# Key stage of an RWKV-7 / GLA trunk: matrix order fixed by hand, head sums on quarters of the array, low-rank results kept on chip

## The chip, the cores and the metric

The kernel runs on one core of a Trainium2 chip. A core has a matrix engine (PE, with its weight loads listed apart as PEld), three elementwise engines (DVE for tensor arithmetic, ACT for activations and copies, POOL), and a queue (SP) from which this kernel issues its DMA transfers. The metric is the device time of one execution in microseconds. Three runs of the kernel before gave 2408.81 to 2409.78 us, median 2409.51 us.

## The reference

Two layers over 272 tokens (16 learned ones and 256 given) of width 2048: RWKV-7 time mixing, then gated linear attention, each followed by a squared-ReLU MLP. The change lies in the first layer, where each of 32 heads has 64 channels:

```python
r = xr @ w_rkv[0]
k = xk @ w_rkv[1]
w_log = -softplus(-(w0 + tanh(xw @ w1) @ w2)) - 0.5
a = sigmoid(a0 + (xa @ a1) @ a2)
kk = hs(k * k_k)                                    # hs: split into heads of 64
kk = kk / maximum(sqrt(sum(kk * kk, axis=-1)), 1e-12)
k = k * (1.0 + (a - 1.0) * k_a)
decay = exp(-exp(hs(w_log)))
y = rwkv7_scan(rh, decay, kh, vh, -kk, kk * ah)
bonus = (sum(rh * kh * r_k, axis=-1, keepdims=True) * vh)
```

Two sums over the 64 channels of a head are needed per token: that of `kk * kk`, which normalizes the key, and that of `rh * kh * r_k`, the bonus.

## The kernel before, in words

Activations are held transposed: 128 channels (two heads) on the partitions, 272 tokens along the row, 16 such tiles. A weight block of 128x1024 float32 is fetched as `raw` (L131, three buffers), split by ACT into a high part `hi` (L137) and by DVE into the rest `lo` (L138), two buffers of each, and used in eight steps of three matmuls (L160 to L162: hi times high part, hi times rest, lo times high part). A projection tile is two blocks, so 48 matmuls into one bank of the accumulator, called `pj` or, for every third tile of keys, `pry`.

Stages of the first layer: receptance (`r`) projections; between them, for each tile, the low-rank results (function `lora`: two small matmuls, L468 and L469, two sigmoids, a scan), which are written to a DRAM tensor `cad` and read back in the key stage (`ca`, L565); then the key stage, the loop over 16 tiles; then the value projections with the chunked recurrence interleaved.

In the key stage a tile f does this. PE makes the 48 matmuls. ACT makes `kk` (key times k_k, L569), its square `sq` (L570), two exponentials `W` and `iW` of the scanned decay (L567, L568), and `kn` (L571). PE sums `sq` over the heads with a 128x128 block matrix of ones, `bones` (L573, into `pm`); ACT takes logarithm and exponential of that (L574, L575); DVE normalizes (L577) and fills, by `put`, the two slots of the tiles `bk` and `ar` (two buffers each): slot 0 of `ar` from `kk`, slot 1 from `r` times `W`, slot 0 of `bk` from `kn`, slot 1 from `kk`. These go to DRAM (`bkd`, L583; `ard`, L586). DVE makes r times k times r_k (L584), PE sums it (L588, into `pu`), ACT copies the sum over `r` (L589). After tile 7 the first 256 columns of tiles 0 to 7 come back as `BK0` and `AR0` (`fetch`, L504), from tile 10 on `scores` multiplies them (L518), with masks on DVE, and after tile 13 `invert`, some 60 dependent DVE operations (`upd`, `sysA`), solves the triangular systems.

The order: outside the blocks marked `manual_schedule` a scheduler lays out every engine's instructions ahead of time, by priority (weight loads first, then program order) and its own estimates of readiness; each engine then runs its list strictly in that order, and waits where an operand is late. In the key stage before, all engines are laid out so, PE too. In the value stage PE's order is written by hand.

Of the kernel before, what the change touches and what calls it, by code (L numbers as in the profile page):

```python
# [11 lines left out]
F32R = mybir.dt.float32r  # L12
# [42 lines left out]
class Kern:  # L55
# [235 lines left out]
    def rwkv(self, done):  # L291
# [193 lines left out]
        tc.keep_in_program_order(nc.scalar.preload_act_table_set("natural_log_exp_and_others"))  # L485
# [4 lines left out]
        nc.gpsimd.memset(Wf[:, 0:1], 1.0)  # L490
        W = Wf[:, 1:]
# [68 lines left out]
        for f in range(KT):  # L560
            r = rr[f]
# [4 lines left out]
            iW, kk, sq, kn = (self.t(ep, [P, T], n, 2) for n in ("iW", "kk", "sq", "kn"))  # L566
            nc.scalar.activation(W, ca[:, 0], AF.Exp, scale=-DECAY)  # L567
            nc.scalar.activation(iW, ca[:, 0], AF.Exp, scale=DECAY)  # L568
            nc.scalar.mul(self.two(kk), ps, self.vec("k_k", f))  # L569
            nc.scalar.activation(sq, kk, AF.Square)  # L570
            nc.scalar.activation(kn, ca[:, 1], AF.Identity, scale=self.vec("k_a", f), bias=self.omka[:, f : f + 1])  # L571
            ss = self.pm()[:, :T]
            nc.tensor.matmul(ss, self.bones, sq, start=True, stop=True)  # L573
            nc.scalar.activation(sq, ss, AF.Ln, bias=self.tiny)  # L574
            nc.scalar.activation(sq, sq, AF.Exp, scale=-0.5)  # L575
            tt(self.two(kn), ps, self.two(kn))
            nc.vector.scalar_tensor_tensor(out=kk, in0=sq, scalar=1e12, in1=kk, op0=ALU.min, op1=ALU.mult)  # L577
            put(ar, 0, kk, Wf[:, :T], 1)
            nc.vector.tensor_copy(ar[:, 0:513:128], kk[:, ::C])
            tt(kk, kk, ca[:, 1])  # L580
            put(bk, 1, kk, iW)
            put(bk, 0, kn, iW)
            nc.sync.dma_start(bkd[f], bk)  # L583
            nc.vector.scalar_tensor_tensor(out=kn, in0=r, scalar=self.vec("r_k", f), in1=kn, op0=ALU.mult, op1=ALU.mult)  # L584
            put(ar, 1, r, W)
            nc.sync.dma_start(ard[f], ar)  # L586
            rk = self.pu()[:, :T]
            nc.tensor.matmul(rk, self.bones, kn, start=True, stop=True)  # L588
            nc.scalar.copy(r, rk)  # L589
            nc.vector.tensor_copy(WC[:, f], W[:, C - 1 : 4 * C : C])  # L590
            if f == 0:
                xv = mix(3, self.xp)
                early2.close()
                wl = ExitStack()
                lp = wl.enter_context(tc.tile_pool(name="wl", bufs=1, reuse_waits="tile"))
                BKs, ARs = ([self.t(lp, [P, 8, 256], n)] for n in ("BK0", "AR0"))
                AMs, AMrs = [self.t(lp, [P, 2, 16, 128], "AM0")], []
                sysA = self.t(lp, [P, 32, 32], "sysA")
                t11 = sysA.rearrange("p a b -> p (a b)")[64:96].rearrange("p (c h s) -> p c h s", c=2, h=16)
                nc.gpsimd.memset(sysA, 0.0)  # L600
            if f == 7:
                fetch(0, BKs, bkd)
                fetch(0, ARs, ard)
            if 9 < f < 14:
                scores(0, (f - 10) // 2, f % 2)
            if f == 13:
                inv = invert(0)
            if f > 13:
                for _ in range(6):
                    next(inv, None)  # L610
# [4 lines left out]
        BKs.append(self.t(kp, [P, 8, 320], "BK1"))  # L615
# [269 lines left out]
        units1 = ((2, 0), (2, 1), (3, 0), (3, 1), (4, 0))  # L885
        self.split_parts = 2
        for i in ((0, 128), (128, 320)):
            fetch(1, BKs, bkd, i)
# [417 lines left out]
```

## Time and profile before

| | us |
|---|---|
| median of three runs | 2409.51 |
| profiled execution, its own time | 2414.07 |
| span of its profile | 2412.3 |
| PE busy in the span | 2364.2 |
| DVE busy | 1636.8 |
| ACT busy | 1239.3 |
| PE busy from 157 to 291 us (the key stage) | 123.87 of 134.00 |
| DVE busy there | 110.91 |
| ACT busy there | 89.79 |

A page of the profile lists each engine's busy time, the chain of work that ended last, the costliest groups of instructions, and the DMA issues. Timeline rows give the start, the length and the engine of single instructions, and in brackets the engine's idle time before one and what ended it. Since matmuls overlap in the pipeline, their cost on PE is read from start to start, not from their lengths. A float32 matmul appears as two records.

### The profile page before, as it was taken

What the parts mean: (1) busy time and instruction counts of PE and PEld (TensorE: products, weight loads), DVE (VectorE), ACT (ScalarE), POOL (GpSimd) and SP (SyncE); (2) the same over time, 40 slices, a digit from 0 to 9 for tenths busy, and PEclk for the clock granted to TensorE, in tenths of its full rate; (3) what the DMA queues carried; (4) which work ended last, traced back from release to release, by engine and by line L of the source; (5) the groups of instructions that cost most, each with busy time, mean ns of one, the idle gap of its engine ahead of it and who ended that gap; (6) DMA issues with size and microseconds to landing.
All of it is one profiled execution on the core that took longest, in us unless ns stands there. A gap on an engine that the chain in (4) does not pass through costs nothing.

```text
span 2412.3 us, 47144 instructions
## 1 busy us (share of the span) xinstructions
PE 2364.2 (98%) x19257; PEld 2233.8 (93%) x19257; DVE 1636.8 (68%) x2742; ACT 1239.3 (51%) x1951; POOL 6.6 (0%) x20
## 2 busy tenths in 40 slices
PE   9999999899999999999999999999999999999998
PEld 8888888789999999999999989998999999999997
DVE  8777886858655555555556788778766666666666
ACT  6366544456555445445445565545555545445444
POOL 0000000000000000000000000000000000000000
PEclk9999999999999999999999999999999999999999
DMA  6578765534555655555555554555666666666665
GB/s 211 170 233 284 240 191 147 148 88 155 183 192 188 190 191 189 188 191 192 187 190 192 182 172 161 166 166 180 197 201 201 201 202 201 202 201 201 201 201 172
DMA packets 160729, 455.29 MB, mean 189 GB/s; under 512 B 34112, under 2 KB 50624, under 8 KB 160512
## 3 DMA queue, kind: packets, MB, share of 16 engines
q1 hardware_dynamic: 160512, 452.27, 58.2%
q8 instruction: 151, 2.47, 0.4%
q14 instruction: 66, 0.54, 0.1%
HBM read 433.86 MB, written 18.35 MB: 187 GB/s over the span
## 4 chain that ended last, share of the span: by engine, by line
PE 70%; DVE 3%; ACT 1%; issue 0%; DVEq 0%; ACTq 0%
PE pj L189 23%; PE pj L160 12%; PE pj L162 12%; PE pj L161 12%; PE pj L190 11%; DVE lo L138 1%; PE pt L1091 0%; DVE sg L1150 0%; ACT hi L137 0%; PE pu L1103 0%; PE pt L1123 0%; DVE cum L1027 0%; DVE fin L1213 0%; PE pu L1104 0%; DVE cj L200 0%
## 5 line engine op out<-in xcount | busy, mean ns | idle before, releaser
L137 ACT CAST hi<-raw 128x1024 fp32r<-128x1024 f32 (+1 forms) x818 | 794.5, 979 | 951.4 <-PE pj L161 514.9
L138 DVE TENSOR_TENSOR lo<-raw,hi 128x1024 fp32r<-128x1024 f32 (+1 forms) x818 | 926.5, 1139 | 518.8 <-ACT hi L137 510.2
L160 PE MATMUL pj<-x,hi 128*128 128x272 f32 x2240 | 642.0, 287 | 5.7 <-DVE cj L200 4.0
L162 PE MATMUL pj<-x,lo 128*128 128x272 f32 x2240 | 629.1, 281 | 4.6 <-DVE lo L138 4.3
L161 PE MATMUL pj<-x,hi 128*128 128x272 f32 x2240 | 628.3, 280 | 0.2 <-DVE x L233 0.2
L189 PE MATMUL pj<-x,hi 128*128 128x512 f32 x1664 | 550.0, 384 | 2.3 <-DVE cj L200 1.3
L190 PE MATMUL pj<-x,lo 128*128 128x256 f32 x1664 | 455.8, 274 | 2.3 <-DVE lo L138 2.2
L160 PEld LDWEIGHTS pj<-x,hi 128*128 128x128 f32 x2240 | 424.2, 189 | 13.7 <-issue 3.7
L162 PEld LDWEIGHTS pj<-x,lo 128*128 128x128 f32 x2240 | 424.4, 189 | 8.0 <-DVE lo L138 7.3
L161 PEld LDWEIGHTS pj<-x,hi 128*128 128x128 f32 x2240 | 424.5, 190 | 3.6 <-issue 1.4
L189 PEld LDWEIGHTS pj<-x,hi 128*128 128x128 f32 x1664 | 315.4, 190 | 46.0 <-ACT hi L137 2.9
L189 PE MATMUL pj<-h,hi 128*128 128x512 f32 x1008 | 330.3, 382 | 0.0
L190 PEld LDWEIGHTS pj<-x,lo 128*128 128x128 f32 x1664 | 320.1, 192 | 6.8 <-DVE lo L138 6.3
L160 PE MATMUL pj<-h,hi 128*128 128x272 f32 (+1 forms) x1040 | 290.1, 279 | 0.0
L161 PE MATMUL pj<-h,hi 128*128 128x272 f32 (+1 forms) x1040 | 290.1, 279 | 0.0
L162 PE MATMUL pj<-h,lo 128*128 128x272 f32 (+1 forms) x1040 | 290.1, 279 | 0.0
L190 PE MATMUL pj<-h,lo 128*128 128x256 f32 x1008 | 274.8, 273 | 0.0
L189 PEld LDWEIGHTS pj<-h,hi 128*128 128x128 f32 x1008 | 190.5, 189 | 26.4
L160 PEld LDWEIGHTS pj<-h,hi 128*128 128x128 f32 x1040 | 196.6, 189 | 0.0
L161 PEld LDWEIGHTS pj<-h,hi 128*128 128x128 f32 x1040 | 196.6, 189 | 0.0
L162 PEld LDWEIGHTS pj<-h,lo 128*128 128x128 f32 x1040 | 196.6, 189 | 0.0
L190 PEld LDWEIGHTS pj<-h,lo 128*128 128x128 f32 x1008 | 193.5, 192 | 0.0
(268 smaller groups left out, 2110.5 us busy)
## 6 DMA issues: line engine op xcount, KB each, us to landing
raw<-mlp_w_d SPq DMA_DIRECT2D x512, 512.0 KB, 4.2
raw<-gla_in_d SPq DMA_DIRECT2D x98, 512.0 KB, 3.4
raw<-w_rkv_d SPq DMA_DIRECT2D x80, 512.0 KB, 4.1
raw<-gla_o_d SPq DMA_DIRECT2D x32, 512.0 KB, 4.2
raw<-w_r_d SPq DMA_DIRECT2D x16, 512.0 KB, 3.4
raw<-rw_oQ_d SPq DMA_DIRECT2D x16, 512.0 KB, 3.4
ard<-ar SPq DMA_DIRECT2D x16, 288.0 KB, 3.6
bkd<-bk SPq DMA_DIRECT2D x16, 288.0 KB, 4.3
```

The costliest lines, as they stand in the source:

```text
L137: nc.scalar.copy(hi[:, h], raw[:, h])
L138: nc.vector.tensor_tensor(out=lo[:, h], in0=raw[:, h], in1=hi[:, h].bitcast(F32), op=ALU.subtract)
L160: nc.tensor.matmul(out, hi[:, ws], xh, start=first, stop=False)
L161: nc.tensor.matmul(out, hi[:, ws], xl, start=False, stop=False)
L162: nc.tensor.matmul(out, lo[:, ws], xh, start=False, stop=last)
L189: nc.tensor.matmul(wide, hi[:, ws], xt, start=kt == 0, stop=False)
L190: nc.tensor.matmul(one, lo[:, ws], xt[:, 0], start=False, stop=kt == nk - 1)
```

## The change

1. In `lora` the results of tiles 0 to 7 are written straight into `hres`, an on-chip tensor that is free at that time; `cad` is written for tiles 8 to 15 alone, and each of these is read into `hres` by a transfer that tile f - 8 of the key stage issues.
2. The mixed input of the values is computed into `d` during the last receptance tiles, its split (`hl`) stays at key tile 1.
3. PE's order in the key stage is written by hand: first half of tile f's projection, the sums for tile f - 1 and f - 2, second half of tile f.
4. `sums` replaces the two 128x128 sums: for each of `sq` (of tile f - 1) and `kn` (of tile f - 2) two matmuls with 64x64 corners of `bones`. Those of `sq` lie on the array's two diagonal quarters, those of `kn` on the other two, so that the heads of `rk` come out swapped and two half copies put them back.
5. `W` gets two buffers; the copies into `ar` and `WC` move from DVE to ACT.
6. `store` writes the tiles 4 to 7 into `BK0`, `AR0` and `BK1` on chip; tiles 0 to 3 are fetched in three transfers after tiles 5, 6 and 7. `BK1` lies in a pool that is open by then, and its later fetch is gone. `scores` and `invert` start one tile earlier.

```diff
-            st = self.t(ep, [P, 2, T], "ca", 2)
+            st = hres[:, 2 * f : 2 * f + 2] if f < NR else self.t(ep, [P, 2, T], "ca", 2)
...
-            nc.sync.dma_start(cad[f], st.rearrange("p a t -> p (a t)"))
+            if f >= NR:
+                nc.sync.dma_start(cad[f], st.rearrange("p a t -> p (a t)"))
...
+            if f == KT - 2:
+                for kt in range(KT):
+                    mixed(d[:, kt], kt, 3)
...
-        Wf = self.t(ep, [P, T + 1], "W")
+        Wfs = [self.t(ep, [P, T + 1], "W", 2) for _ in range(2)]
...
+        def store(f, dst, x, i):
+            if 3 < f < 8:
+                nc.sync.dma_start((BKs, ARs)[i][0][:, f], x[:, :256])
+                nc.sync.dma_start(dst[f][:, 256:] if i else BKs[1][:, f], x[:, 256:])
+            else:
+                nc.sync.dma_start(dst[f], x)
...
+        def sums(sq):
+            ss, last = self.pm()[:, :T] if sq is not None else None, held.pop() if held else None
+            todo = [(sq, ss, 0)] if sq is not None else []
+            if last:
+                r, kn = last
+                rk = self.pu()[:, :T]
+                todo.append((kn, rk, 1))
+            for x, out, i in todo:
+                for q in range(2):
+                    nc.tensor.matmul(out[half(q ^ i)], self.bones[half(q), half(q)], x[half(q)], start=True, stop=True)
+            if last:
+                for q in range(2):
+                    nc.scalar.copy(r[half(q)], rk[half(1 - q)])
+            return ss
...
-            ps = self.proj(pair(wk, f), xk, T, bank=self.pry if f % 3 == 2 else None)
-            ca = self.t(ep, [P, 2, T], "ca", 2)
-            nc.sync.dma_start(ca.rearrange("p a t -> p (a t)"), cad[f])
...
+        def rest(f):
+            r, Wf = rr[f], Wfs[f % 2]
...
+            ca = hres[:, 2 * i : 2 * i + 2]
...
+            ss = sums(sq)
...
+            put(ar, 1, r, W)
...
+            held.append((r, kn))
...
-            nc.vector.tensor_copy(ar[:, 0:513:128], kk[:, ::C])
+            nc.scalar.copy(ar[:, 0:513:128], kk[:, ::C])
+            store(f, ard, ar, 1)
...
+            if f < NR:
+                nc.sync.dma_start(ca.rearrange("p a t -> p (a t)"), cad[f + NR])
+            store(f, bkd, bk, 0)
+            nc.scalar.copy(WC[:, f], W[:, C - 1 : 4 * C : C])
...
+        with tc.manual_schedule(engines={ENG.PE}):
+            for f in range(KT + 1):
+                if f < KT:
+                    ps = (self.pry if f % 3 == 2 else self.pj)()[:, :T]
+                    keyproj(f, ps, 0)
+                if f:
+                    rest(f - 1)
+                if f < KT:
+                    keyproj(f, ps, 1)
+                    front(f, ps)
...
+                if f in (5, 6, 7):
+                    dst, src, i, j = ((BKs[0], bkd, 0, 256), (ARs[0], ard, 0, 256), (BKs[1], bkd, 256, 576))[f - 5]
+                    nc.sync.dma_start(dst[:, :4], src[:4, :, i:j].rearrange("f p n -> p f n"))
+                if 8 < f < 13:
+                    scores(0, (f - 9) // 2, (f + 1) % 2)
+                if f == 12:
+                    inv = invert(0)
...
+            sums(None)
```

PE's list before, in the first half of key tile 5 (`pry`), with `sq` of tile 4:

```order
L160 MATMUL pry_2362<-x_1209,hi_2365 128x272
L161 MATMUL pry_2362<-x_1209,hi_2365 128x272
L162 MATMUL pry_2362<-x_1209,lo_2366 128x272
L573 MATMUL pm_2339<-sq_2332,cst_125 128x272
L160 MATMUL pry_2362<-x_1210,hi_2365 128x272
```

The sum stood after the fifth of the tile's sixteen groups of three; that over `kn` of the same tile stood inside the ninth. PE's list now, at the second half of key tile 5 (`pry`); the sums stand in the middle of the 48 matmuls, `pm` with `sq` of tile 4 and `pu` with `kn` of tile 3:

```order
L160 MATMUL pry_2308<-x_1212,hi_2311 128x272
L161 MATMUL pry_2308<-x_1212,hi_2311 128x272
L162 MATMUL pry_2308<-x_1212,lo_2312 128x272
L584 MATMUL pm_2343<-sq_2305,cst_125 64x272 x2
L584 MATMUL pu_2344<-kn_2243,cst_125 64x272 x2
L160 MATMUL pry_2308<-x_1213,hi_2375 128x272
L161 MATMUL pry_2308<-x_1213,hi_2375 128x272
L162 MATMUL pry_2308<-x_1213,lo_2376 128x272
```

Before, each tile had one instruction of each kind with 128 rows, at a place that the scheduler chose; now four of 64 rows stand together, at the same place in every tile.

DVE's list before, from the normalizing of key tile 4 (`kk_2331`) on; `ar_1791` is the buffer of tiles 3 and 5, `r_20` is the receptance of tile 5:

```order
L577 SCALAR_TENSOR_TENSOR kk_2331<-sq_2332,kk_2331 128x272
L293 TENSOR_TENSOR ar_1790<-kk_2331,W_1796 128x4x64
L293 TENSOR_TENSOR ar_1790<-kk_2331,W_1796 128x15
L579 COPY ar_1790<-kk_2331 128x5
L138 TENSOR_TENSOR lo_2461<-raw_2458,hi_2460 128x1024
L293 TENSOR_TENSOR kk_2331<-kk_2331,ca_2328 128x272
L293 TENSOR_TENSOR ar_1791<-r_20_94,W_1796 128x4x64
L293 TENSOR_TENSOR bk_1788<-kk_2331,iW_2330 128x4x64
L293 TENSOR_TENSOR bk_1788<-kk_2331,iW_2330 128x16
L293 TENSOR_TENSOR ar_1791<-r_20_94,W_1796 128x16
L590 COPY WC_105<-W_1796 128x4
L138 TENSOR_TENSOR lo_2491<-raw_2488,hi_2490 128x1024
```

The first write into the buffer of tile 3 for tile 5 (`ar_1791` from `r_20`) stood behind tile 4's normalizing, a whole tile's row of work after tile 3's.

DVE's list now, from the last products of tile 2 (`kk_2110`, which was stored from buffer `ar_1790`) to the normalizing of tile 3 (`kk_2207`); `r_19` is the receptance of tile 4, which uses `ar_1790` again:

```order
L293 TENSOR_TENSOR kk_2110<-kk_2110,hres_72 128x272
L293 TENSOR_TENSOR bk_1788<-kk_2110,iW_2145 128x4x64
L293 TENSOR_TENSOR bk_1788<-kk_2110,iW_2145 128x16
L138 TENSOR_TENSOR lo_2277<-raw_2274,hi_2276 128x1024
L293 TENSOR_TENSOR kn_2243<-pj_2114,kn_2243 128x272
L293 TENSOR_TENSOR ar_1790<-r_19_93,W_1796 128x4x64
L293 TENSOR_TENSOR bk_1789<-kn_2243,iW_2242 128x4x64
L293 TENSOR_TENSOR bk_1789<-kn_2243,iW_2242 128x16
L293 TENSOR_TENSOR ar_1790<-r_19_93,W_1796 128x16
L620 SCALAR_TENSOR_TENSOR kn_2243<-r_18_92,vecs_126,kn_2243 128x272
L138 TENSOR_TENSOR lo_2312<-raw_2309,hi_2311 128x1024
L622 SCALAR_TENSOR_TENSOR kk_2207<-sq_2208,kk_2207 128x272
```

The slot from `r` of tile 4 is now written ahead of tile 3's normalizing, into the buffer that tile 2 has just stored: between that store and this write stand three products, one weight split and one more product. The two small copies are gone from this list.

ACT's list now, in the low-rank stage, where `hres` takes the results of tiles 0 to 2 and `x` is the mixed input of the keys:

```order
L471 ACTIVATE iW_1301<-pm_1297,vecs_126 128x272
L329 CAST x_1220<-xm_1281 128x272
L472 ACTIVATE hres_72<-pry_1298,vecs_126 128x272
L614 ACT_TABLE_LOAD
L614 ACTIVATE W_1796<-hres_72 128x272
L471 ACT_TABLE_LOAD
L471 ACTIVATE iW_1311<-pm_1307,vecs_126 128x272
L137 CAST hi_1410<-raw_1408 128x1024
L472 ACTIVATE hres_72<-pry_1308,vecs_126 128x272
```

The exponential `W` of key tile 0 has moved up between the sigmoids, which need another table of functions: a table load stands on either side of it. The same happens once more for tile 1. Before, this stage had no table load.

More of the change, by code (lines that the diff above doesn't have):

```diff
@@ L488, in rwkv @@
             nc.gpsimd.memset(x[:, 512:], 0.0)
-        Wf = self.t(ep, [P, T + 1], "W")
-        nc.gpsimd.memset(Wf[:, 0:1], 1.0)
-        W = Wf[:, 1:]
+        Wfs = [self.t(ep, [P, T + 1], "W", 2) for _ in range(2)]
+        for x in Wfs:
+            nc.gpsimd.memset(x[:, 0:1], 1.0)
         def put(dst, slot, a, b, skip=0):
@@ new lines, in rwkv @@
+        held, tiles = [], {}
+        half = lambda q: slice(HEAD * q, HEAD * q + HEAD)
+        def sums(sq):
[12 more added lines that the diff above has]
+            return ss
@@ new lines, in keyproj, with front @@
+        def keyproj(f, ps, half):
+            hi, lo = self.wload(pair(wk, f)[half])
+            for j in range(8):
+                kt = 8 * half + j
+                self.mm3(ps, hi, lo, slice(j * P, (j + 1) * P), xk[kt][:, 0], xk[kt][:, 1], kt == 0, kt == KT - 1)
+        def front(f, ps):
+            kk, sq = (self.t(ep, [P, T], n, 2) for n in ("kk", "sq"))
+            ps = self.back(ps)
+            nc.scalar.mul(self.two(kk), ps, self.vec("k_k", f))
+            nc.scalar.activation(sq, kk, AF.Square)
+            tiles[f] = ps, kk, sq
@@ new lines, in rest @@
+        def rest(f):
+            r, Wf = rr[f], Wfs[f % 2]
+            W = Wf[:, 1:]
+            bk, ar = st2[0][f % 2], st2[1][f % 2]
+            ps, kk, sq = tiles.pop(f)
+            i = f % NR
+            ca = hres[:, 2 * i : 2 * i + 2]
+            iW, kn = (self.t(ep, [P, T], n, 2) for n in ("iW", "kn"))
+            nc.scalar.activation(kn, ca[:, 1], AF.Identity, scale=self.vec("k_a", f), bias=self.omka[:, f : f + 1])
+            tt(self.two(kn), ps, self.two(kn))
+            ss = sums(sq)
@@ L567, in rwkv @@
             nc.scalar.activation(W, ca[:, 0], AF.Exp, scale=-DECAY)
             nc.scalar.activation(iW, ca[:, 0], AF.Exp, scale=DECAY)
[L569 to L573, printed above, removed]
             nc.scalar.activation(sq, ss, AF.Ln, bias=self.tiny)
@@ L580, in rwkv @@
+            store(f, ard, ar, 1)
             tt(kk, kk, ca[:, 1])
             put(bk, 1, kk, iW)
[L582 to L610, printed above, removed]
+            if f < NR:
+                nc.sync.dma_start(ca.rearrange("p a t -> p (a t)"), cad[f + NR])
+            store(f, bkd, bk, 0)
+            nc.scalar.copy(WC[:, f], W[:, C - 1 : 4 * C : C])
@@ new lines, in rwkv @@
+        with tc.manual_schedule(engines={ENG.PE}):
[8 more added lines that the diff above has]
+                    front(f, ps)
+                if f == 1:
+                    xv = [self.t(self.xp, [P, 2, T], "x", KT, F32R) for _ in range(KT)]
+                    for kt in range(KT):
+                        hl(xv[kt], d[:, kt])
+                    early2.close()
+                    wl = ExitStack()
+                    lp = wl.enter_context(tc.tile_pool(name="wl", bufs=1, reuse_waits="tile"))
+                    BKs, ARs = ([self.t(lp, [P, 8, 256], n)] for n in ("BK0", "AR0"))
+                    BKs.append(self.t(lp, [P, 8, 320], "BK1"))
+                    AMs, AMrs = [self.t(lp, [P, 2, 16, 128], "AM0")], []
+                    sysA = self.t(lp, [P, 32, 32], "sysA")
+                    t11 = sysA.rearrange("p a b -> p (a b)")[64:96].rearrange("p (c h s) -> p c h s", c=2, h=16)
+                    nc.gpsimd.memset(sysA, 0.0)
+                if f in (5, 6, 7):
[5 more added lines that the diff above has]
+                    inv = invert(0)
+                if f > 12:
+                    for _ in range(6):
+                        next(inv, None)
+            sums(None)
@@ L887, in rwkv @@
         for i in ((0, 128), (128, 320)):
-            fetch(1, BKs, bkd, i)
             fetch(1, ARs, ard, i)
```

7 lines of the change are left out of this document (2 added, 5 removed).

## The prediction

> **What bounds the kernel now.** I read the page first (busy times, the chain), then the waits of the key stage, the timeline around single sums, and the stage by windows.
>
> ```profile
> PE 2364.2 (98%) x19257; PEld 2233.8 (93%) x19257; DVE 1636.8 (68%) x2742; ACT 1239.3 (51%) x1951; POOL 6.6 (0%) x20
> PE 70%; DVE 3%; ACT 1%; issue 0%; DVEq 0%; ACTq 0%
> ```
>
> PE is busy for 98% of the span and carries the chain. So a change pays where it takes an instruction off PE or ends a wait of PE, and costs where it makes PE wait. The rows that follow, of the waits from 157 to 300 us (the key stage and its end: wait, us in total, times, longest), show what PE waits for:
>
> ```profile
> PE pm L573 <- ACT sq L570: 5.7, 7, 1.4
> ...
> PE pt L518 <- DMA BK<-bkd: 2.3, 1, 2.3
> ...
> PE pu L588 <- DVE kn L584: 1.2, 3, 0.9
> ```
>
> Two of the three are the head sums, which stand where PE arrives before ACT or DVE has made their operand; the third is the fetch. Together 9.2 us. The windows (PE, PEld, DVE, ACT, POOL busy, clock, DMA share, GB/s) say how far the others are from their limits:
>
> ```profile
> 200.00:220.00 20.00, 18.68 (x142) 17.45 (x141) 16.36 (x46) 14.56 (x28) 0.00 (x0) 1.00 0.82 269
> 220.00:240.00 20.00, 17.47 (x139) 16.35 (x138) 12.53 (x25) 10.93 (x19) 0.00 (x0) 0.96 0.90 301
> ```
>
> A tile lasts 7.0 us there (its sum L573 starts at 202.07 us, that of the next tile at 209.06, rows below); DVE works 16.36/20x7.0 = 5.7 us of it, ACT 5.1. DMA is at 0.82 and, with the fetch, at 0.90. Nothing has much room if a tile comes down towards 6.4 us, and this is what I weigh below.
>
> **The change part by part.** *Head sums.* A timeline from 201.66 us (start, length), around one tile's two sums, with the next tile's L573 at its end:
>
> ```profile
> 201.66 0.28 PE L162 MATMUL pj<-x,lo 128*128 128x272 f32 x1
> 202.07 0.73 PE L573 MATMUL pm<-sq,cst 128*128 128x272 f32 x2
> ...
> 202.75 0.28 PE L161 MATMUL pj<-x,hi 128*128 128x272 f32 x1
> ...
> 203.79 0.28 PE L161 MATMUL pj<-x,hi 128*128 128x272 f32 x1
> 203.92 0.72 PE L588 MATMUL pu<-kn,cst 128*128 128x272 f32 x2
> ...
> 204.59 0.28 PE L160 MATMUL pj<-x,hi 128*128 128x272 f32 x1
> ...
> 209.06 0.50 PE L573 MATMUL pm<-sq,cst 128*128 128x272 f32 x1
> ```
>
> Projection matmuls start every 0.115 us (two steps: 0.23). L573 lengthens the distance of its neighbours (there is one more L160 between) to 202.75-201.66 = 1.09, so it costs 0.86 us; L588 costs 204.59-203.79-0.23 = 0.57. Sixteen tiles x 1.43 = 22.9 us. Afterwards 17 groups (the first has `sq` alone, the last `kn` alone) have four 64x64 products. Whether four quarters run beside one another is shown by the recurrence, which uses them:
>
> ```profile
> 385.73 0.37 PE L715 MATMUL pu<-S,AR 64*64 64x64 f32 x1
> 385.73 0.37 PE L713 MATMUL pry<-AR,S 64*64 64x64 f32 x1
> 385.74 0.37 PE L715 MATMUL pu<-S,AR 64*64 64x64 f32 x1
> 385.75 0.37 PE L713 MATMUL pry<-AR,S 64*64 64x64 f32 x1
> ```
>
> Four products start within 20 ns, two into `pu` and two into `pry`, just the new pattern. So a group should cost about one pass of 272 columns. Its bounds are 0.57 (L588 as a whole) and the group of half-array products nearest to it:
>
> ```profile
> 310.62 0.28 PE L162 MATMUL pj<-x,lo 128*128 128x272 f32 x1
> 310.83 1.16 PE L518 MATMUL pt<-AR,BK 64*128 64x128 f32 x16
> ...
> 312.15 0.28 PE L161 MATMUL pj<-x,hi 128*128 128x272 f32 x1
> ```
>
> 312.15-310.62-0.23 = 1.30 us. I take 0.9, the dearer of today's single sums, since weights of four small matrices are loaded: 17x0.9 = 15.3, a gain of 7.6 us (bounds 13.2 and 0.8).
>
> [...]
>
> *Fixed order.* The sums stand after 24 matmuls (24x0.115 = 2.8 us) of the next tile. ACT has in that time `kk` and `sq` and perhaps a weight's `hi`, about 2.2 us by their rows; `kn` gets a whole tile more. I take away the two sum waits and, because the 1.0 MB fetch after tile 7 becomes three pieces whose last is issued two tiles ahead of `scores`, the third: 9.2 us (bounds 6.9, should the fetch still be late, and 9.2).
>
> *Clock.* The third wait had a sequel:
>
> ```profile
> 235.22 0.28 PE L162 MATMUL pj<-x,lo 128*128 128x272 f32 x1
> 237.77 1.71 PE L518 MATMUL pt<-AR,BK 64*128 64x128 f32 x16 [2.27 <-DMA BK<-bkd]
> ...
> 240.93 0.43 PE L162 MATMUL pry<-x,lo 128*128 128x272 f32 x1
> 241.16 0.43 PE L160 MATMUL pry<-x,hi 128*128 128x272 f32 x1
> ```
>
> L518 took 1.71 instead of 1.16, and the matmuls behind it start every 0.23 us instead of 0.115, until 241.6; granted clock 0.96 there. The loss is 0.55 plus half a dozen steps of 0.115, about 1.3 us, and goes with the gap (bounds 0 and 1.3).
>
> [...]
>
> *Work off and onto the engines.* DVE's groups of the key stage (line, engine, shapes, count | busy, mean ns | idle before, releaser), then an ACT group:
>
> ```profile
> L138 DVE TENSOR_TENSOR lo<-raw,hi 128x1024 fp32r<-128x1024 f32 x31 | 37.9, 1224 | 13.1 <-ACT hi L137 13.0
> L584 DVE SCALAR_TENSOR_TENSOR kn<-r,vecs,kn 128x272 f32<-128x272 f32 x16 | 8.0, 499 | 0.2
> L577 DVE SCALAR_TENSOR_TENSOR kk<-sq,kk 128x272 f32<-128x272 f32 x16 | 7.1, 441 | 3.2 <-ACT sq L575 3.1
> ...
> L293 DVE TENSOR_TENSOR ar<-r,W 128x256 f32<-128x256 f32 x16 | 6.7, 421 | 2.7 <-ACT W L567 2.7
> ...
> L579 DVE COPY ar<-kk 128x5 f32<-128x5 f32 x16 | 2.7, 167 | 0.0
> L590 DVE COPY WC<-W 128x4 f32<-128x4 f32 x16 | 2.6, 165 | 0.0
> ```
>
> ```profile
> L589 ACT COPY r<-pu 128x272 f32<-128x272 f32 x15 | 5.6, 376 | 4.4 <-DVE WC L590 3.3 <-PE pu L588 1.1
> ```
>
> Two copies leave DVE (0.33 us a tile) and, with `r` in two halves (0.38 more), ACT gets about 0.7: DVE 5.4, ACT 5.8 a tile against PE's 48x0.115+0.9 = 6.4. Nothing, then, with 0.6 us of cover; without it, 0.1 us a tile for every 0.1 that ACT is dearer. The values' mix moves to the last receptance tiles, where ACT and DVE are half idle: nothing too. On SP's queue eight writes of `cad` and eight reads of `ca` go away, the late `BK1` fetch as well; the stores of tiles 4 to 7 become two each; the next weights stand behind a tile's stores, but are needed almost two tiles later, against 4 to 5 us to land.
>
> *A loop through `ar`.* Now DVE writes `r` times `W` of tile f+2 into the buffer of tile f, shortly behind its store. If the store hasn't landed, DVE stands, and behind it the weight split and the normalizing of tile f+1, on which the next store depends. The loop is: landing L, the rest of tile f+1's list on DVE (two products into `bk`, one of 16 columns, L584: 1.3 us), a split (1.15 with overlap), L577 (0.44), ACT's copy (0.26 estimated): L+3.2. Landing (KB, median us; first and second row of the whole run, then two of 215 to 250 us, with the fetch):
>
> ```profile
> ard<-ar SPq DMA_DIRECT2D x16, 288.0 KB, 3.6
> ...
> cad<-ca SPq DMA_DIRECT2D x16, 272.0 KB, 5.1
> ```
>
> ```profile
> raw<-w_rkv_d SPq DMA_DIRECT2D x9, 512.0 KB, 5.3
> ...
> ard<-ar SPq DMA_DIRECT2D x2, 288.0 KB, 4.1
> ```
>
> At 3.6 the loop takes 6.8 us against PE's 6.4: 0.4 for each of tiles 1 to 8, 3.2 less about 1 us of slack at its start, some 2 us. Tiles 5 to 7 also move 1.05 MB of weights, 0.59 of stores, 0.28 of `ca` and 0.5 to 0.65 of fetch, 2.5 MB; at 301/0.90 = 334 GB/s that is 7.4 us, 1 us over PE's tile, of which later weights' lead hides a part. I take 4.5 in all (bounds 0, and 8x(5.3-3.2) = 17). Tiles 9 to 12, with `scores` on PE, last 1.3 us longer and absorb it.
>
> *Table loads.* In the low-rank stage the exponentials of tiles 0 and 1 bring four more:
>
> ```profile
> 158.15 1.28 ACT L485 ACT_TABLE_LOAD   x1
> ```
>
> 4x1.28 = 5.1 us on ACT, which has cover there as above, but the sigmoids behind them free the banks of PE's next low-rank products. I take 0.5 (bounds 0 and 5.1).
>
> *Inversion a tile earlier.* It brings some 60 DVE operations beside tiles that had none. From 291 us, where DVE is now fullest, the window, the wait of PE, and the inversion's group (four inversions, with an equal group of sums):
>
> ```profile
> 291.00:336.00 45.00, 42.79 (x401) 40.73 (x400) 42.42 (x99) 16.57 (x34) 0.00 (x0) 1.00 0.79 238
> ```
>
> ```profile
> PE pj L162 <- DVE lo L138: 2.1, 2, 1.1
> ```
>
> ```profile
> L293 DVE TENSOR_TENSOR upd<-sysA 64x30 f32<-64x30 f32 (+29 forms) x120 | 39.1, 326 | 17.3 <-DMA sysA<-sysd 8.8 <-issue 5.9
> ```
>
> One inversion is 2x39.1/4 = 19.6 us of DVE; there DVE is at 94% and PE already lost 2.1. Beside key tiles (DVE 5.4 of 6.4) it falls behind: 19.6 us more in what I count as 45 to 48 us of PE makes 56 of DVE, less what runs on into the value tiles. I take 3.5 (bounds -2.1, should the present wait go, and 6).
>
> The sum: -7.6-9.2-1.3+4.5+0.5+3.5 = -9.6. The profiled execution took 2414.07 us (span 2412.3): 2404.5. It stands 4.56 above the median of 2409.51, so 2400 for the median.
>
> **The rivals.** *Loop and tail don't bite*: the store lands in 3.2 us or less, as it can with fewer `ca` transfers about, and the inversion costs 1. -7.6-9.2-1.3+0.5+1 = -16.6: 2393. For it speaks that DVE idles for 3.6 of 20 us now; against it the 3.6 us of the row.
>
> *The quarters don't run beside one another*, so the change doesn't do what it says: a group costs what two full sums do, 1.43, and 17 of them 24.3, a loss of 1.4 instead of 7.6 gained: -0.6, 2409. Against it stand L713 and L715.
>
> *Tables and tail at their upper bounds*: 5.1 and 6 instead of 0.5 and 3.5: -2.5, 2407. For it: DVE's 94%.
>
> *Slower, through the loop*: the `ar` store lands late over tiles 1 to 8 and 13 to 15, each of which then takes L-3.2 longer than PE needs. The other terms give -7.6-9.2-1.3+0.5+3.5 = -14.1, so it decides from L = 3.2+14.1/11 = 4.5 us. At the 5.1 of the `cad` row: 11x1.9 = 20.9, +6.8, 2416. For it: 4.1 and 5.3 us beside the fetch. Against it: a tile of over 7 us loads the transfers less than now, when the row has 3.6.
>
> **How the numbers follow.** Chances: the forecast 0.50 (2400), loop and tail don't bite 0.17 (2393), tables and tail 0.10 (2407), quarters in turn 0.08 (2409), slower through the loop 0.15 (2416). A difference of 0.2%, 4.8 us, is about what a measurement of this kernel can tell from none, so faster means under 2404.7 and slower over 2414.3. Of the forecast's own 0.50 some 0.06 lies above 2404.7, by the bounds of its DVE terms; the two cases at 2407 and 2409 count as the same but for 0.03 and 0.02 on either side: faster 0.64, same 0.20, slower 0.16. The range goes from 2391, below the second case for a cheaper group, to 2412; outside it lie most of the slower case and a tail below.
>
> **What would show it.** Right: tiles of 6.4 to 6.8 us between 180 and 260; groups of L584 costing about 0.9 us between neighbours; no wait of PE for `sq`, `kn` or the fetch of `BK`, clock 1.00 throughout; three table loads become seven. The loop would show as DVE's `ar` waiting for the DMA `ard<-ar`, with `lo` late for PE behind it; the tail as PE waiting for `lo` from 270 us on. Wrong: quarter products that start one after another, a tile at 7 us or more (the loop, or ACT above 6.4), or waits at L468 and L469 of several us.

## The result and the profile after

The changed kernel took 2404.27 us (median of 13 runs, 2402.02 to 2408.09) against 2410.44 us for the kernel before on the same chips (13 runs, 2408.01 to 2411.84): a ratio of 0.9976, 95% interval 0.9968 to 0.9983. It is 6.2 us faster, 0.24%. The forecast was 2400 from 2409.5, 9.6 us faster, with a range of 2391 to 2412. The total came out near; several of its larger terms did not, and the experiments show which.

The page of the changed kernel. Its profiled execution took 2405.51 us, its span is 2403.6:

```profile
PE 2352.7 (98%) x19321; PEld 2220.0 (92%) x19321; DVE 1633.8 (68%) x2710; ACT 1253.4 (52%) x2003; POOL 6.7 (0%) x21
...
PE 70%; DVE 3%; ACT 1%; DMA 0%; issue 0%; DVEq 0%; ACTq 0%
```

PE has 11.5 us less to do, but the span is only 8.7 us shorter: PE waits more than before. Two places bound the stretch: the last low-rank product (L469), with which the key stage begins, and the first product with an inverse (L641, now L696) after it. From the kernel before:

```profile
156.75 0.39 PE L469 MATMUL pry<-ta,l 96*128 96x272 f32 x1
...
336.71 0.38 PE L641 MATMUL pt<-sysA,AM 32*32 32x32 f32 x12
```

From the changed kernel:

```profile
157.84 0.39 PE L469 MATMUL pry<-ta,l 96*128 96x272 f32 x1
...
332.94 0.34 PE L696 MATMUL pt<-sysA,AM 32*32 32x32 f32 x10
```

Between them 180.0 us have become 175.1: the stage gained 4.9 us, less 1.1 lost ahead of it. (0.9 of the 1.1 is there at 11 us, ahead of all that was changed, and is missing in later kernels with the same change; it belongs to this execution.) The other 4.9 us lie behind 333 us, where the change touches little; I come back to them. The windows of the changed kernel that answer to those of before (PE, PEld, DVE, ACT, POOL busy, clock, DMA share, GB/s):

```profile
200.00:220.00 20.00, 16.95 (x147) 14.91 (x146) 14.93 (x35) 15.25 (x35) 0.00 (x0) 1.00 0.91 294
220.00:240.00 20.00, 18.12 (x168) 16.26 (x167) 16.53 (x39) 13.51 (x32) 0.00 (x0) 1.00 0.78 261
291.00:336.00 45.00, 42.86 (x466) 41.04 (x466) 35.52 (x78) 16.84 (x34) 0.95 (x1) 0.96 0.68 204
```

PE is busy for 16.95 of 20 us from 200 to 220, where it had been for 18.68. The clock no longer falls between 220 and 260, but now between 291 and 336. The waits of 157 to 300 us say why PE idles (us, times, longest):

```profile
ACT ar L624 <- DVE ar L293: 26.3, 15, 4.2
DVE ar L293 <- DMA ard<-ar: 9.6, 9, 3.3
...
PE pm L584 <- ACT sq L600: 7.0, 10, 0.9
...
PE pry L162 <- DVE lo L138: 2.9, 2, 2.5
...
PE pj L162 <- DVE lo L138: 2.3, 2, 1.1
...
PE pu L584 <- DVE kn L620: 1.4, 1, 1.4
```

The waits for `sq` and `kn` that the fixed order was to end are there again, 8.4 us of them; that for the fetch of `BK` is gone. Beside them stand two sorts that were next to nothing before: PE for the weight split `lo` (5.2 us, before none that is listed), and DVE for the landing of the store of `ar` (9.6 us, before 0.3). One turn of that loop, in the timeline of DVE, ACT and PE after a store that SP issued at 183.69 us:

```profile
190.12 0.43 DVE L293 TENSOR_TENSOR ar<-r,W 128x256 f32<-128x256 f32 x1 [3.34 <-DMA ard<-ar]
```

```profile
193.48 0.20 ACT L624 COPY ar<-kk 128x5 f32<-128x5 f32 x1 [4.21 <-DVE ar L293]
```

```profile
192.69 0.38 PE L162 MATMUL pry<-x,lo 128*128 128x272 f32 x1 [2.54 <-DVE lo L138]
...
196.27 0.45 PE L584 MATMUL pm<-sq,cst 64*64 64x272 f32 x2 [0.76 <-ACT sq L600]
```

DVE may write `r` times `W` only when the store has left the buffer, 6.4 us after its issue; the weight split and the normalizing stand behind it; ACT stands at its copy into `ar` until DVE has done both, with the next `hi`, `kk` and `sq` behind that copy. So one late store reaches PE twice, as a late `lo` and as a late `sq`. That PE's waits come from here is tested by the first experiment.

### The profile page after: what moved, and what is told of

Its sections match the earlier page's. It is cut to its first block, busy times and chain, and to the rows that moved or that the text cites. A ratio compares the mean times of both kernels' runs of the same rounds, so it can differ in the third digit from the quotient of the medians.

```text
span 2403.6 us, 47283 instructions
## 1 busy us (share of the span) xinstructions
PE 2352.7 (98%) x19321; PEld 2220.0 (92%) x19321; DVE 1633.8 (68%) x2710; ACT 1253.4 (52%) x2003; POOL 6.7 (0%) x21
## 4 chain that ended last, share of the span: by engine, by line
PE 70%; DVE 3%; ACT 1%; DMA 0%; issue 0%; DVEq 0%; ACTq 0%
PE pj L189 23%; PE pj L160 12%; PE pj L162 12%; PE pj L161 12%; PE pj L190 11%; DVE lo L138 1%; ACT hi L137 0%; PE pt L1145 0%; DVE sg L1204 0%; DMA raw<-mlp_w_d 0%; PE pu L1157 0%; PE pt L1177 0%; DVE cum L1081 0%; DMA raw<-gla_in_d 0%; DVE fin L1267 0%
## 5 line engine op out<-in xcount | busy, mean ns | idle before, releaser
L162 PE MATMUL pj<-x,lo 128*128 128x272 f32 x2240 | 627.5, 280 | 6.9 <-DVE lo L138 6.8
L162 PEld LDWEIGHTS pj<-x,lo 128*128 128x128 f32 x2240 | 424.4, 189 | 9.7 <-DVE lo L138 9.0
L162 PE MATMUL pj<-h,lo 128*128 128x272 f32 (+1 forms) x1040 | 290.1, 279 | 0.0
L162 PEld LDWEIGHTS pj<-h,lo 128*128 128x128 f32 x1040 | 196.6, 189 | 0.0
```

The source lines that it names most:

```text
L162: nc.tensor.matmul(out, lo[:, ws], xh, start=False, stop=last)
```

## The experiments

Medians of five to eight runs (13 for the changed kernel), each with the ratio to runs of the kernel before on the same chip. The runs stem from several sessions, in which the median of the kernel before lay between 2409.54 and 2410.44 us; so the ratios compare better than the times. Their intervals are some 3 us to either side in the smaller samples, and differences of 2 to 5 us between two of these kernels mostly need the traces beside them.

| kernel | us | ratio | 95% interval |
|---|---|---|---|
| changed kernel | 2404.27 | 0.9976 | 0.9968 to 0.9983 |
| ar3: third `ar` buffer | 2396.07 | 0.9932 | 0.9919 to 0.9946 |
| cpdve: copy back on DVE | 2405.85 | 0.9978 | 0.9967 to 0.9988 |
| full: whole sums | 2401.94 | 0.9968 | 0.9955 to 0.9980 |
| invlate: inversion as before | 2403.86 | 0.9970 | 0.9960 to 0.9980 |
| ar3full: ar3 and whole sums | 2392.78 | 0.9934 | 0.9921 to 0.9946 |
| ar3apart: ar3, whole sums apart | 2393.44 | 0.9930 | 0.9917 to 0.9944 |
| early: ar3full, sums earlier | 2398.01 | 0.9952 | 0.9939 to 0.9966 |
| ar3slow: ar3, half the steps | 2392.82 | 0.9930 | 0.9918 to 0.9943 |
| ar3refetch: ar3, AR1 twice | 2401.71 | 0.9970 | 0.9960 to 0.9981 |
| ar3bk: ar3, 1.3 MB beside | 2397.96 | 0.9946 | 0.9934 to 0.9959 |
| ar3cad: ar3, cad for all tiles | 2398.69 | 0.9951 | 0.9938 to 0.9965 |
| best: ar3full, late first step | 2391.59 | 0.9924 | 0.9912 to 0.9936 |

### What holds the key tiles: the store or ACT's copy

```diff
-        st2 = [[self.t(ep, [P, 576], n, 2) for i in range(2)] for n in ("bk", "ar")]
+        st2 = [[self.t(ep, [P, 576], n, k) for i in range(k)] for n, k in (("bk", 2), ("ar", 3))]
...
-            bk, ar = st2[0][f % 2], st2[1][f % 2]
+            bk, ar = st2[0][f % 2], st2[1][f % 3]
```

> A third buffer for ar (the staging of the low-rank results of tiles 8 to 15 moves into the still unused bk buffers to make the room); the copy of ar stays on ACT. Theory A (the landing of the ar store holds DVE): DVE's 9.6 us of waits for ard<-ar go, and with them PE's waits for lo in the key stage (2.5, 1.1, 1.1, 0.3) and most of the ten waits for sq (7.0); key tiles of 6.4 us, 2392 to 2395 us against 2404 for the changed kernel. Theory B (ACT's copy of ar stands ahead of the next hi, kk and sq and waits for DVE, which then waits for hi): the waits for the DMA and for lo go, but the waits of PE for sq stay at 0.3 to 0.5 us each, tiles of 6.8, 2397 to 2400.

The second experiment puts the copy back on DVE:

```diff
-            nc.scalar.copy(ar[:, 0:513:128], kk[:, ::C])
+            nc.vector.tensor_copy(ar[:, 0:513:128], kk[:, ::C])
```

> The small copy into ar goes back from ACT to DVE; all else as in the changed kernel. Theory B (ACT's copy closes a ring between ACT, DVE and PE): the waits of PE for sq go (7.0 us), the waits of DVE for hi too, those for the DMA ard<-ar stay; 2397 to 2401 us. Theory A (the landing of the store alone): no gain, DVE has 0.17 us a tile more to do, 2404 to 2407.

The third buffer gave 2396.07, 1 us above the range of theory A, and 8.2 us less than the changed kernel (10.6 by the ratios); the copy on DVE gave nothing. (The edit that makes room for it, the staging of tiles 8 to 15 in `bk`, isn't shown.) The waits of 157 to 300 us with three buffers:

```profile
ACT ar L624 <- DVE ar L293: 11.5, 16, 2.3
...
PE pm L584 <- ACT sq L600: 4.0, 3, 1.9
...
DVE ar L293 <- DMA ard<-ar: 0.3, 1, 0.3
```

The wait for the store is gone (0.3 us), those for `lo` are too, and of ten waits for `sq` three are left, two of them behind 260 us, beside the inversion. The copy is still on ACT here. So theory A holds: it was the landing. The store now lands later, and costs nothing. The DMA row (count, KB, median us to landing) of the changed kernel, and that with three buffers:

```profile
ard<-ar SPq DMA_DIRECT2D x12, 288.0 KB, 3.2
```

```profile
ard<-ar SPq DMA_DIRECT2D x12, 288.0 KB, 3.9
```

cpdve is the weaker half of the test. There ACT's next instruction, `W` for tile f+2, waits for the same DVE product instead (23.7 us in all, 14 times), so that the order on ACT was not really loosened. That the ring over ACT would cost something with a store that lands in time is excluded by ar3, not by cpdve.

### What the quarters are worth

```diff
-                for q in range(2):
-                    nc.tensor.matmul(out[half(q ^ i)], self.bones[half(q), half(q)], x[half(q)], start=True, stop=True)
+                nc.tensor.matmul(out, self.bones, x, start=True, stop=True)
```

> The head sums as before the change, two 128x128 matmuls with the whole block matrix and one copy back, at the place of the fixed order. If PE's work sets the time of every tile: 17 groups go from 0.83 to about 1.43 us, +10 us, 2414. If a ring of waits (theory A or B) sets ten of the seventeen tiles, the dearer sums lie in PE's idle time there: +4 us or less, 2405 to 2408.

2401.94 us: no slower than with quarters (intervals of the ratio overlap), and below both ranges. That fits the ring, but the trace shows something else as well. A group on quarters that waits for nothing, in the changed kernel:

```profile
171.85 0.28 PE L162 MATMUL pry<-x,lo 128*128 128x272 f32 x1
172.06 0.45 PE L584 MATMUL pm<-sq,cst 64*64 64x272 f32 x2
172.07 0.45 PE L584 MATMUL pu<-kn,cst 64*64 64x272 f32 x2
172.34 0.40 PE L584 MATMUL pm<-sq,cst 64*64 64x272 f32 x2
172.35 0.40 PE L584 MATMUL pu<-kn,cst 64*64 64x272 f32 x2
172.68 0.38 PE L160 MATMUL pry<-x,hi 128*128 128x272 f32 x1
172.90 0.28 PE L161 MATMUL pry<-x,hi 128*128 128x272 f32 x1
```

and two whole sums at the same place of the same tile, in full:

```profile
170.77 0.28 PE L162 MATMUL pry<-x,lo 128*128 128x272 f32 x1
170.89 0.62 PE L583 MATMUL pm<-sq,cst 128*128 128x272 f32 x2
171.35 0.62 PE L583 MATMUL pu<-kn,cst 128*128 128x272 f32 x2
171.61 0.48 PE L160 MATMUL pry<-x,hi 128*128 128x272 f32 x1
171.92 0.28 PE L161 MATMUL pry<-x,hi 128*128 128x272 f32 x1
```

The four quarters do run beside one another: `pm` and `pu` start 10 ns apart, in two passes 0.28 us apart. From L162 to the second matmul behind they cost 172.90-171.85-0.23 = 0.82 us. The whole sums start 0.46 us apart and cost, between the same two, 171.92-170.77-0.23 = 0.92. So the quarters save 0.1 us a tile, under 2 us in all, not 0.6. Their two passes are worth what was hoped, 0.28 us each for four products, where the two whole sums need 0.92 for their four passes; but 0.26 of the 0.82 lies ahead of them and behind. The weight load of the next projection matmul stands still behind the group:

```profile
172.68 0.19 PEld L160 LDWEIGHTS pry<-x,hi 128*128 128x128 f32 x1 [0.41 <-issue]
```

A wait of 0.4 us of this kind stands behind each of the 17 groups in the kernels with quarters (7.0 us in all in the changed kernel and in ar3), and behind no sum in those with whole ones. Runs on the kernel without the loop, where PE sets the time, put that to the test:

> Three ar buffers, and the two head sums as whole 128x128 matmuls side by side at the place of the fixed order. Without the waits of the changed kernel PE sets the time of the key tiles, so the sums' own cost shows. Theory C (what makes a sum dear is a lone full-precision matmul among the others; two that stand together cost 0.94 us against 0.83 on quarters): 17x0.11 = +1.9 us over three buffers with quarters, 2398. Theory Q (the quarters halve the sums): 1.43 against 0.83, +10 us, 2406.

```diff
+        def sum2(n=2):
+            if len(held) >= n:
+                r, kn = held.pop(0)
+                nc.scalar.copy(r, sum1(kn, self.pu))
...
             for j in range(8):
+                if half and j == 2:
+                    sum2()
                 kt = 8 * half + j
```

> Three ar buffers, and the two head sums as whole matmuls that stand apart, the key's in the middle of the tile and the bonus's six matmuls later. Theory C: 0.86 and 0.57 as before the change, 1.43 a tile against 0.94 together, +8 us over the two together and +10 over the quarters, 2406. Theory Q: the same time as the whole matmuls side by side, within 2 us.

Whole sums side by side 2392.78 (ratio 0.9934), whole sums six matmuls apart 2393.44 (0.9930), quarters 2396.07 (0.9932): no difference that the intervals show. (The quarters' 1.7 us also stand against waits: PE waits 4.8 us for `sq` and `kn` in ar3, 2.4 in ar3full.) Theory Q falls by ar3full, 2392.78 instead of 2406, and theory C by ar3apart, 2393.44 instead of 2406: a lone sum isn't dear either. With its operand there in time it costs 0.46 us, by the rows of ar3apart:

```profile
196.42 0.28 PE L162 MATMUL pj<-x,lo 128*128 128x272 f32 x1
196.53 0.62 PE L577 MATMUL pm<-sq,cst 128*128 128x272 f32 x2
196.79 0.48 PE L160 MATMUL pj<-x,hi 128*128 128x272 f32 x1
197.11 0.28 PE L161 MATMUL pj<-x,hi 128*128 128x272 f32 x1
```

197.11-196.42-0.23 = 0.46, where L573 before the change, in the same surroundings, cost 0.86. The difference stands on the weight loads. In ar3apart the load of the sum starts with the matmul ahead; before the change it waits for `sq`, although the row of the matmul itself shows no wait:

```profile
196.42 0.30 PEld L577 LDWEIGHTS pm<-sq,cst 128*128 128x128 f32 x2
```

```profile
202.07 0.30 PEld L573 LDWEIGHTS pm<-sq,cst 128*128 128x128 f32 x2 [0.33 <-ACT sq L570]
```

The kernel before itself holds the counter-example, one tile in which `sq` came in time and the weight load did not wait:

```profile
179.42 0.28 PE L160 MATMUL pj<-x,hi 128*128 128x272 f32 x1
179.53 0.63 PE L573 MATMUL pm<-sq,cst 128*128 128x272 f32 x2
...
180.12 0.28 PE L162 MATMUL pj<-x,lo 128*128 128x272 f32 x1
```

```profile
179.44 0.30 PEld L573 LDWEIGHTS pm<-sq,cst 128*128 128x128 f32 x2
```

180.12-179.42-0.23 = 0.47, the same instruction, in the same kernel, at 0.4 us less.

Whether the place makes this was tried by placing the pair where the key's sum stood before, after 15 matmuls (1.7 us) instead of 24 (the main lines of the edit):

```diff
+                if half == 0 and j == 5 and f:
+                    rest(f - 1)
                 kt = 8 * half + j
```

> Three ar buffers and whole sums side by side, but the sums stand after 15 of the tile's 48 matmuls (1.7 us) instead of 24 (2.8 us), where the key's sum stood before the change. Theory P (the place decides: the operand sq is just late there, and the wait, part of which shows on PE's weight loads alone, is what made the sums before dear): waits for sq on the weight loads in most of the tiles, 0.5 to 1 us each, +7 to +15 us over the same kernel with the sums in the middle, 2400 to 2408. Theory S (the sums' own cost is what it is, wherever they stand): 2392 to 2394.

2398.01 us, ratio 0.9952 against 0.9934: 5.2 us slower than the same sums in the middle by the times, 4.3 by the ratios, whose intervals overlap a little. It lies between the two ranges. The waits of early, of 157 to 300 us, and one of its pairs:

```profile
PEld pm L583 <- ACT sq L600: 6.3, 12, 1.0
PE pm L583 <- ACT sq L600: 3.8, 11, 0.8
```

```profile
177.64 0.28 PE L162 MATMUL pj<-x,lo 128*128 128x272 f32 x1
178.22 0.73 PE L583 MATMUL pm<-sq,cst 128*128 128x272 f32 x2 [0.31 <-ACT sq L600]
...
179.36 0.28 PE L161 MATMUL pj<-x,hi 128*128 128x272 f32 x1
```

The pair, one of eight alike, costs 179.36-177.64-0.23 = 1.49 us there. Of the 0.57 over 0.92 the matmul's row shows 0.31 as a wait; the rest is the weight load's, which sums to 6.3 us where PE's sums to 3.8. From 228 to 252 us, where `scores` lengthens the tiles and `sq` has more time, four pairs at the same place wait for nothing and cost 0.92 (229.43-228.28-0.23). So theory P has the mechanism, at less than I gave it (+7): it is the late operand that makes a sum dear, the place is worth 4 to 5 us, and part of a wait for an operand is seen on PEld alone. (DVE's list changes a little there as well, the normalizing ahead of a weight split, so that not all of the time need be the place.)

### The inversion

```diff
-                if f == 12:
+                if f == 13:
                     inv = invert(0)
-                if f > 12:
+                if f > 13:
```

> The inversion of the first block begins after tile 13 as before the change, not after tile 12; the scores stay a tile earlier. If the earlier inversion costs PE waits for lo in the tail (the prediction's +3.5): 2400 to 2402 us. If the earlier inversion is what shortens the value stage (its results land 2 us late for PE instead of 4.8, and the clock stays up): 2407 to 2410, with PE's waits for AM<-invd back.

2403.86 us against 2404.27: neither. On the changed kernel it does not matter when the inversion begins. On the kernel without the loop two more runs looked for what is left in the last key tiles:

```diff
-                    for _ in range(6):
+                    for _ in range(3):
```

> Three ar buffers, and the first inversion takes three steps in each of key tiles 13 to 15 instead of six, the rest later. If the inversion's operations beside the last key tiles are what makes PE wait there (sq 3.5, kn 0.8 us with three buffers): these waits halve, -2 us, 2394. If they move into the value tiles, where DVE is as full: 2396, with waits for lo after 291 us instead.

2392.82, ratio 0.9930 against 0.9932. The sum wait stays (PE for `sq` 3.5 us against 4.0 over the key stage). What stands ahead of it is not the number of steps but the first one, `upd`, which waits 1.4 to 1.7 us for `sysA` in DVE's list (ar3, ar3full, ar3slow), ahead of a tile's normalizing. So the last run has whole sums, and fetches `sysA` after tile 12 but takes the first step a tile later:

```diff
                     inv = invert(0)
-                if f > 12:
+                    next(inv)
+                if f > 13:
```

> Three ar buffers, whole sums side by side, and the inversion's input fetched after tile 12 but its first step made a tile later, so that no DVE operation of a key tile stands behind the wait for sysA (1.45 us before tile 12's normalizing with three buffers and whole sums, PE's two waits for sq of 1.1 and 1.3 us behind it). If that wait is the cause of the last tiles' waits: both go, 2390 to 2391. If the inversion's operations themselves are: one of them stays, 2392 to 2393.

2391.59 us, ratio 0.9924 (0.9912 to 0.9936), 0.9934 without it: 1.2 us less by the times, 2.4 by the ratios, which the intervals don't separate. The waits shrink (PE's for `sq` from 2.4 us) but don't go (157 to 300 us):

```profile
PE pm L583 <- ACT sq L598: 1.7, 2, 0.9
...
DVE upd L293 <- DMA sysA<-sysd: 0.9, 1, 0.9
```

It has the lowest median of the kernels here, though ar3full and ar3slow are not separated from it: 18 us under the kernel before, 12.5 under the changed one by the ratios, and it has no quarters in it.

### The other two parts

The low-rank results of tiles 0 to 7 still go to `hres`, but are also written to `cad` and read back in the key stage, on three buffers:

```diff
-            if f >= NR:
+            if True:
                 nc.sync.dma_start(cad[f], st.rearrange("p a t -> p (a t)"))
...
+                if f < NR:
+                    nc.sync.dma_start(hres[:, 2 * f : 2 * f + 2].rearrange("p a t -> p (a t)"), cad[f])
```

> Three ar buffers, and the low-rank results of tiles 0 to 7 are also written to cad and read back to hres in the key stage, so that eight writes in the low-rank stage and eight reads more stand on the queue. If keeping them on chip was worth time beside the loop: waits of ACT for hres and slower stores, 2397 to 2400. If it was hidden: within 1 us of three buffers, 2392 to 2396.

2398.69, ratio 0.9951 against 0.9932: 2.6 us more by the times, 4.6 by the ratios, whose intervals overlap. The trace says where. Not in the stores, as I had expected: PE's wait for `sq` stays at 3.7 us. The last low-rank product (L469) comes at 159.57 us instead of 156.83, and PE waits 1.5 us at L468 for a sigmoid; these 2.7 us are about what the two spans differ by (2.6). So, by one trace, this part is worth time in the stage where the writes went away. But the kernel before had these writes and reached that point at 156.75: what they cost depends on what else stands there, and on what is not shown.

For the late transfer of `BK1`, which is gone, two runs moved as many bytes again:

> Three ar buffers, and after the key stage the transfer of AR1 runs twice, so that 1.3 MB is moved there as before the change, when BK1 came back too. If the missing transfer is why the value stage is some 2 to 4 us shorter than before: the waits for AM<-invd or sysA<-sysd grow and the time goes to 2398 to 2400. If not: 2396, within 1 us.

2401.71 us, in neither range, with one wait of PE of 8.0 us for `AR<-ard`. That run tells of its own edit only: the scores wait for the doubled transfer of `AR1` itself. Into a spare place instead:

> Three ar buffers, and after the key stage 1.3 MB more are moved, in two pieces like BK1 before the change, into a spare place that nothing waits for (the run that doubled AR1 itself had made the scores wait 8 us for it and so told nothing of this). If the missing BK1 transfer is why the value stage from 340 to 460 us is 2 to 4 us shorter: 2397 to 2400 us, PE's wait for AM<-invd back at 4 to 5 us. If it isn't: the time of three buffers, 0.993 of before, 2392 to 2396.

2397.96 us, ratio 0.9946 against 0.9932, intervals that overlap. The time lies in the range of the first case, but not by its mechanism: where the run loses, it is at 290 us, where PE waits 2.8 us for `AR1`; PE's wait for `AM<-invd` is 2.6 us, not the 4.8 of the kernel before. So the transfer is not what shortened the value stage.

## Why the prediction was right, and where it was not

**What bounds the kernel.** Right: PE carries the chain before and after, and only its instructions and waits counted. From the last low-rank product to the first with an inverse they add up: -9.0 us of sums (next paragraph) and +4.4 of waits, 13.6 where 9.2 had been, make -4.6, and -4.9 was measured. Forecast for the same stretch, with clock, loop and tail, was -10.1; the 4.9 us behind it, which nothing in the forecast gives, make up for most of that. That the total came so near is in good part luck.

**Head sums, -7.6.** By its own arithmetic the term was met: 17 groups at 0.82 us (0.9 forecast) make 13.9 us instead of the 22.9 before, -9.0. Its reason was wrong. The 0.86 us of L573 were taken for the cost of the instruction; they held a wait of its weight load (0.33 us). A sum whose operand is there costs 0.46, two 0.92, four quarters 0.82. The quarters themselves are worth under 2 us, and nothing that the runs show (ar3full and ar3 have the same ratio within their intervals). The rest of the 9.0 is the place in the order, at which the operand is there in time; of that, early gives back 4 to 5.

**The quarters run beside one another** rather than in turn: right, L584's rows, `pm` and `pu` 10 ns apart. The two products of `sq` share one row of two records, 0.45 us long where a single record takes 0.39 at the least, so the two start within 0.06 us, and the passes of all four products follow each other after 0.28.

**Fixed order, -9.2.** Wrong in the changed kernel, and outside its bounds: only the fetch's 2.3 us went, and 8.4 us of waits for `sq` and `kn` and 5.2 for `lo` stand in place of 9.2. The step that failed is that ACT would have 2.8 us for 2.2 us of work: it counted the length of ACT's list (by ACT's rows of the kernel before `kk`, `sq` and `hi` are 0.48, 0.43 and 1.04 us, 1.95 in all) and not what ACT waits for in it, the copy into `ar`, behind DVE, behind a store. Without the loop the order does nearly what was forecast: three waits for `sq` and one for `kn` are left, 4.8 us, most of it beside the inversion.

**The loop through ar, +4.5.** The mechanism was right, and named with its sign (`ar` waiting for `ard<-ar`, a late `lo` behind it). The term was mis-sized: taking the loop away gives 8 to 11 us. The forecast took the median landing, 3.6 us, which afterwards was 3.2; but the late landings set the wait, 3.3 us at the longest, and each is felt twice, through `lo` and through `sq`. Of the rival that this loop makes the kernel slower, the mechanism was right and the price too high.

**Clock, -1.3.** The gap at 237 us is gone, and the clock is 1.00 from 157 to 291 us (0.99 before); but behind another gap, of 2.1 us, it is 0.55 from 316 to 318 us (0.56 from 238 to 240 before), with the same spacing of 0.23 us. About as much was lost there as gained: net nothing.

**Table loads, +0.5.** They are there, four more of 1.28 us, and hidden: the low-rank products of L468 take 46.4 us from first to last (110.93 to 157.28) where they took 47.0.

**Inversion, +3.5.** Not shown. On the changed kernel, where the loop sets the key tiles, beginning it a tile later changes nothing (2403.86), and PE's wait for `lo` in the value tiles is 2.1 us as before. What it may cost without the loop is DVE's stand at `sysA`, 1.2 us by the times of the last run, which the intervals don't show.

**Not foreseen.** 4.9 us behind 333 us. All kernels tried have some 1 to 5 us of it, invlate and ar3bk too, so it comes neither from the earlier inversion nor from the missing transfer. The traces say where it lies: 3.3 us between 363 and 410 us, the rest before 508. The lead of the changed kernel on the same products is 3.8 us at 363 and 7.1 us at 410, and ar3, full and invlate gain the same 3.3 us over the kernel before on that stretch. What stands there in the kernel before is this wait, and behind it a granted clock of 0.91 from 380 to 400 us, where the changed kernel has no wait and 1.00:

```profile
382.69 1.19 PE L651 MATMUL pt<-AM,rs 32*32 32x32 f32 x62 [1.28 <-DMA AM<-invd]
```

Why the inverse comes in time afterwards is not shown. The kernel before has one trace here, of an execution 4.6 us above its median of three (3.6 above that of thirteen), the changed kernel's 1.2 above its own; so part of it may belong to that one execution. It stays open.

## What to carry to other kernels

Price an instruction only from an occurrence whose operands were early: look at the weight-load rows beside the matmul's, since a wait there, 0.33 us here, lengthened the matmul's interval (0.86 us against 0.46) without being put down as its wait. When work is moved ahead, look for the buffer that it writes: here two buffers that sufficed at one distance from their store (0.3 us of waits) became a loop at a shorter one (9.6 us), and a third buffer was worth 8 to 11 us, a finer use of the array under 2. And give a list of an engine not only its length, but also the instruction in it that waits for another engine.

## What was not expected of the hardware

Behind some gaps of PE of about 2 us the granted clock is lower, behind others of the same length it is not. After a wait of 2.14 us in the changed kernel the matmuls start every 0.23 us for a while (granted clock 0.55 from 316 to 318 us):

```profile
313.62 0.38 PE L162 MATMUL pj<-x,lo 128*128 128x272 f32 x1 [2.14 <-DVE lo L138]
...
314.28 2.02 PE L522 MATMUL pt<-AR,BK 64*128 64x128 f32 x16
...
317.06 0.43 PE L160 MATMUL pj<-x,hi 128*128 128x272 f32 x1
317.29 0.43 PE L161 MATMUL pj<-x,hi 128*128 128x272 f32 x1
...
317.89 0.28 PE L161 MATMUL pj<-x,hi 128*128 128x272 f32 x1
```

The granted clock of 291 to 336 us is 0.96 there, as it is with gaps of 2.12 us in cpdve and 1.64 in early. It is not lower behind 2.54 us at 190 in the changed kernel (1.00 from 180 to 200 us), nor behind 2.06 in ar3 or 2.10 in full (1.00 in the same window). The plainest pair is ar3apart and ar3full: a gap of 2.23 us at 301 us in both, 0.96 in one and 1.00 in the other. The slow stretch lasts some 3.5 us (314.28 to 317.74 in the changed kernel). So a term for the clock behind a gap of 2 us is a chance of about 1.5 us, by my estimate from these numbers (3.5 us at 0.23 instead of 0.115 us a step, and 0.96 of 45 us is 1.8 us lost), not a sum to count on in either direction. What decides whether a gap has such a stretch behind it isn't shown.
